# The key's norm, squared and on one side only, in an RWKV-7 and gMLP step

## The chip, the cores and the metric

The kernel runs on one core of one Trainium2 chip. The metric is the device time of one execution in microseconds (us), lower is better; the time before is the median of three runs. The engines are named as the profile names them: PE is TensorE (its weight loads are PEld), DVE is VectorE, ACT is ScalarE, POOL is GpSimd, SP is the engine that issues most DMAs.

## The reference

One layer of a backbone over 512 latent tokens and 128 context tokens, 2048 wide, in fp32: a modulated RMSNorm, one projection `w_in`, a bidirectional RWKV-7 time mixing on one half of the channels and a chunked gMLP on the other, `w_out`, and a SwiGLU feed-forward part. The change lies in the time mixing, in how the key `kk` is normalized for each head of 64 channels:

```python
kk = heads(k * lp['k_k'])
kk = kk * lax.rsqrt(jnp.maximum(jnp.sum(kk * kk, axis=-1, keepdims=True), 1e-24))
for d in range(2):
    decay = heads(jnp.exp(-jnp.exp(w_log)))
    a = jax.nn.sigmoid(lp['a0'][d] + ad @ lp['a2'][d])
    kd = heads(k * (1.0 + (a - 1.0) * lp['k_a']))
    y, s_fin = _delta_scan(rh, decay, kd, vh, -kk, kk * heads(a), s0[:, d], reverse=(d == 1))
# a step of the scan, with a_t = -kk and b_t = kk * a:
#   sa = S a_t ;  S = S * w_t + sa b_t^T + v_t k_t^T ;  y_t = S r_t
```

The normalized key enters the state only as the product of a reading (`S a_t`) and a writing (`sa b_t^T`) of the same token, so one factor of it can be moved from the one to the other.

## The kernel before, in words

All 640 tokens are columns of tiles with 128 channels on the partitions, so a tile of one channel block is 128x640. The kernel has four stages: modulation and norm; `w_in` with the preparation of both mixers; the recurrence over chunks of 64 tokens with `w_out`; and the feed-forward part, which is the longest. Big matmuls are fp32 split into a high and a low part, three matmuls for each block (L190 to L192), 320 columns wide; the high part is cast on ACT (L168), the low part subtracted on DVE (L169).

The change lies in the second stage. Blocks of 128 output columns of `w_in` come one after another, each in four pieces. When a block is done, `take` copies it to SBUF (L955) and puts a generator for it into the queue `mixA`: `take_r`, `take_v` and `take_k` for each of eight pairs of heads, `take_gv` and `take_gu` for each gMLP group. `between` is called after the matmuls of a block row and runs the queue by a budget. Each `yield x` of a generator says that x units of the budget are used up; how fast the queue is run follows from the cost that is still outstanding (`pace`, with `KCOST` = 50 for a `take_k`). Two more queues hold the solving of small triangular systems (`solve`, `merge`).

`take_k` does the following for a pair: it takes the shifted key `zk`, multiplies it by `k_k` into `nkk` (L565), squares that on ACT (L567), sums the squares of each head with a matmul by a matrix of ones (`pmm`, L519), bounds the sums from below (`ssq`, L570), takes the square root on ACT (L572) and the reciprocal on DVE in two halves (L576), and multiplies `nkk` by -1 and that (L578). Then, for each direction `d`, TensorE makes the low-rank products `pwa` (L592, L593), ACT their tanh (`sg` and `tha`, L596), DVE a running sum of `sg` (`L`, L604), ACT the exponentials of it (L607, L608). The reading rows `R` are `nkk` and `zr` times the exponential (L615, L618, L621); the writing rows `X` are `tha` times `nkk` (L632) and the key `f` times the inverse exponential (L636 to L640). TensorE multiplies them chunk by chunk into `pG` (L651), DVE masks the result into `GR` and `GA` (L660, L661), ACT copies part of it to `GB` (L655, L663), TensorE transposes `X` (`pXT`, L669; copies `XT`, L675) and makes `pW0` (L683). At the end `zv` is weighted by another product through `pmm` (L698). All of it goes to DRAM in `d_S` for the recurrence.

`nkk`, `ssq` and the others have one buffer each, apart from `t1` with two. The order of instructions on an engine follows the text only loosely: it is set when the program is built.

## Time and profile before

| | us |
|---|---|
| time, median of 3 runs (lowest to highest) | 3225.3 (3222.83 to 3228.34) |
| the profiled execution: time | 3226.49 |
| the profiled execution: span from first to last instruction | 3224.7 |
| TensorE busy | 3097.7 |
| VectorE busy | 2337.3 |
| ScalarE busy | 1460.7 |
| mean granted clock of TensorE | 0.990 |

The profile is of one execution. A line like `L572 ACT ACTIVATE ssq<-ssq x8: 737/740/742` gives the line of the kernel, the engine, the operation, the tile written and the tiles read, how many there were, and the shortest, median and longest duration in ns. In a list of waits, `PE pG L651 <- DVE X L636: 5.1, 8, 1.6` says that PE, ahead of the matmuls of L651 into `pG`, stood idle until DVE had written `X` in L636: 5.1 us in total, 8 times, 1.6 us at the longest.

### The profile page before, as it was taken

What the parts mean: (1) busy time and instruction counts of PE and PEld (TensorE: products, weight loads), DVE (VectorE), ACT (ScalarE), POOL (GpSimd) and SP (SyncE); (2) the same over time, 40 slices, a digit from 0 to 9 for tenths busy, and PEclk for the clock granted to TensorE, in tenths of its full rate; (3) what the DMA queues carried; (4) which work ended last, traced back from release to release, by engine and by line L of the source; (5) the groups of instructions that cost most, each with busy time, mean ns of one, the idle gap of its engine ahead of it and who ended that gap; (6) DMA issues with size and microseconds to landing.
All of it is one profiled execution on the core that took longest, in us unless ns stands there. A gap on an engine that the chain in (4) does not pass through costs nothing.

```text
span 3224.7 us, 72310 instructions
## 1 busy us (share of the span) xinstructions
PE 3097.7 (96%) x28216; PEld 2861.5 (89%) x28216; DVE 2337.3 (72%) x4107; ACT 1460.7 (45%) x3197; POOL 1215.7 (38%) x1065
## 2 busy tenths in 40 slices
PE   6999999999999999999999999999999999999997
PEld 4688778777878888899999999999999999999997
DVE  4547666676666677767877777778788688777778
ACT  3334444444444444346644444444444454444365
POOL 2001121211122023311366556656655645555542
PEclk9999999999999999999999999999999999999999
DMA  9667786777778688564534433343344364553453
GB/s 372 220 197 203 194 215 187 204 205 197 201 197 220 193 273 268 178 197 128 149 112 125 121 117 118 117 128 120 107 130 128 104 197 151 157 157 111 145 167 121
DMA packets 740438, 550.88 MB, mean 171 GB/s; under 512 B 141056, under 2 KB 673504, under 8 KB 731264
## 3 DMA queue, kind: packets, MB, share of 16 engines
q1 hardware_dynamic: 727136, 532.47, 55.5%
q0 software_dynamic: 10624, 13.23, 1.7%
q8 instruction: 222, 3.64, 0.5%
q14 instruction: 120, 0.98, 0.1%
q10 hardware_dynamic: 2336, 0.57, 0.1%
HBM read 437.79 MB, written 110.95 MB: 170 GB/s over the span
## 4 chain that ended last, share of the span: by engine, by line
PE 72%; DVE 10%; DMA 8%; issue 5%; ACT 3%; POOL 2%; SPq 0%; DVEq 0%; POOLq 0%; ACTq 0%
PE P L1640 15%; PE P L1638 15%; PE P L1639 15%; PE big L190 5%; PE big L192 4%; PE big L191 4%; DVE lo L1420 2%; DMA wt<-in_w_mod_dram 2%; PE pm L903 1%; PE pG L651 1%; DMA raw<-in_w_in_dram 1%; PE big L1035 1%; PE big L1479 1%; PE big L1478 1%; PE big L1480 1%
## 5 line engine op out<-in xcount | busy, mean ns | idle before, releaser
L1640 PE MATMUL P<-xo,lo 128*128 128x320 f32 x2352 | 727.9, 310 | 2.2 <-DVE lo L1420 2.1
L1638 PE MATMUL P<-xo,hi 128*128 128x320 f32 x2352 | 727.5, 309 | 0.7 <-ACT hi L1419 0.7
L1639 PE MATMUL P<-xo,hi 128*128 128x320 f32 x2352 | 727.4, 309 | 0.0
L1420 DVE TENSOR_TENSOR lo<-raw,hi 128x512 fp32r<-128x512 f32 x526 | 512.0, 977 | 164.8 <-ACT hi L1419 160.3
L1419 ACT CAST hi<-raw 128x512 fp32r<-128x512 f32 x526 | 327.7, 623 | 487.6 <-PE P L1639 393.5
L190 PE MATMUL big<-h_hi,hi 128*128 128x320 f32 x1376 | 450.4, 327 | 10.1 <-ACT hi L168 6.7
L1640 PEld LDWEIGHTS P<-xo,lo 128*128 128x128 f32 x2352 | 442.1, 188 | 3.2 <-DVE lo L1420 2.9
L1638 PEld LDWEIGHTS P<-xo,hi 128*128 128x128 f32 x2352 | 442.0, 188 | 1.0 <-ACT hi L1419 1.0
L1639 PEld LDWEIGHTS P<-xo,hi 128*128 128x128 f32 x2352 | 442.0, 188 | 0.0
L192 PE MATMUL big<-h_hi,lo 128*128 128x320 f32 x1376 | 433.8, 316 | 0.8 <-DVE lo L169 0.6
L191 PE MATMUL big<-h_lo,hi 128*128 128x320 f32 x1376 | 431.7, 314 | 0.5 <-DVE h_lo L352 0.5
L1548 POOL TENSOR_TENSOR raw<-raw 128x512 f32<-128x512 f32 x252 | 406.6, 1623 | 16.4 <-DVE lo L1420 4.9
L1640 PE MATMUL P<-xd,lo 128*128 128x320 f32 x1232 | 384.9, 312 | 16.3 <-DVE lo L1420 16.3
L1638 PE MATMUL P<-xd,hi 128*128 128x320 f32 x1232 | 383.4, 311 | 1.8 <-ACT hi L1419 1.1
L1639 PE MATMUL P<-xd,hi 128*128 128x320 f32 x1232 | 382.1, 310 | 0.0
L190 PEld LDWEIGHTS big<-h_hi,hi 128*128 128x128 f32 x1376 | 261.9, 190 | 79.0 <-issue 47.8
L169 DVE TENSOR_TENSOR lo<-raw,hi 128x512 fp32r<-128x512 f32 x268 | 183.3, 687 | 195.0 <-ACT hi L168 177.7
L1419 ACT CAST hi<-rawd 128x512 fp32r<-128x512 f32 (+1 forms) x288 | 168.7, 589 | 241.9 <-PE P L1639 201.7
L192 PEld LDWEIGHTS big<-h_hi,lo 128*128 128x128 f32 x1376 | 261.3, 190 | 9.5 <-issue 2.8
L191 PEld LDWEIGHTS big<-h_lo,hi 128*128 128x128 f32 x1376 | 261.8, 190 | 6.0 <-DVE h_lo L352 1.2
L168 ACT CAST hi<-raw 128x512 fp32r<-128x512 f32 x268 | 164.9, 619 | 223.8 <-PE big L191 115.8
L1640 PEld LDWEIGHTS P<-xd,lo 128*128 128x128 f32 x1232 | 232.4, 189 | 22.9 <-DVE lo L1420 22.7
(404 smaller groups left out, 6046.4 us busy)
## 6 DMA issues: line engine op xcount, KB each, us to landing
wt<-in_w_mod_dram SPq DMA_DIRECT2D x96, 1024.0 KB
raw<-in_w_ffn_gate_dram SPq DMA_DIRECT2D x182, 256.0 KB
raw<-in_w_ffn_up_dram SPq DMA_DIRECT2D x182, 256.0 KB
rec<-d_S SPq DMA_DIRECT2D x80, 576.0 KB
raw<-in_w_in_dram SPq DMA_DIRECT2D x172, 256.0 KB
rawd<-in_w_ffn_down_dram SPq DMA_DIRECT2D x128, 256.0 KB
raw<-in_w_out_dram SPq DMA_DIRECT2D x96, 256.0 KB
xd<-d_os SPq DMA_DIRECT2D x66, 320.0 KB
```

The costliest lines, as they stand in the source:

```text
L168: S.copy(hi, raw)
L169: V.tensor_sub(lo, raw, hi.bitcast(F32))
L190: TE.matmul(halves[hf], hi[:, k, :], h_hi[:, kb, s], start=(kb == 0), stop=False)
L191: TE.matmul(halves[hf], hi[:, k, :], h_lo[:, kb, s], start=False, stop=False)
L192: TE.matmul(halves[hf], lo[:, k, :], h_hi[:, kb, s], start=False, stop=(kb == KB - 1))
L651: in_turn([lambda cc=cc, h=h: TE.matmul(two[h][:, cc - c0, :], X[hsl(h), cc].rearrange("p s t -> p (s t)"), R[hsl(h), cc].rearrange("p s t ...
L1419: S.copy(hi[:, 0:nk], raw[:, 0:nk])
L1420: V.tensor_sub(lo[:, 0:nk], raw[:, 0:nk], hi[:, 0:nk].bitcast(F32))
L1548: G.tensor_tensor(out=o[:, 0:nk], in0=p[:, 0:nk], in1=q[:, 0:nk], op=ALU.subtract)
L1638: TE.matmul(ps, hi[:, k, :], xk[:, 0, :], start=f, stop=False)
L1639: TE.matmul(ps, hi[:, k, :], xk[:, 1, :], start=False, stop=False)
L1640: TE.matmul(ps, lo[:, k, :], xk[:, 0, :], start=False, stop=l)
```

## The change

The square root is left out, with its yield of 0.5. `nkk` takes the factor -1 at once and is not normalized; the reading rows use it as it is. The reciprocal is now that of the squared norm, and a new tile `nks` holds `nkk` times it; the writing rows use `nks` in place of `nkk`.

```diff
-        V.tensor_scalar_mul(nkk, zk, prm[:, C_KK + p:C_KK + p + 1])
+        V.tensor_scalar(nkk, zk, prm[:, C_KK + p:C_KK + p + 1], -1.0, op0=ALU.mult, op1=ALU.mult)
         sq = bk.tile([P, T], F32, tag="t1", name="sqk", bufs=2)
         S.activation(sq, nkk, AF.Square)
         yield 0.5
         ssq = bp.tile([P, T], F32, tag="t2", name="ssq", bufs=1)
         pmm([(bones, sq)], lambda ps, s: V.tensor_scalar_max(ssq[:, s], ps, 1e-24))
         yield 1.0
-        S.activation(ssq, ssq, AF.Sqrt)
-        yield 0.5
         for hf in range(2):
             s = slice(HALF * hf, HALF * hf + HALF)
             V.reciprocal(ssq[:, s], ssq[:, s])
             yield 2.0
-        V.scalar_tensor_tensor(out=nkk, in0=nkk, scalar=-1.0, in1=ssq, op0=ALU.mult, op1=ALU.mult)
+        nks = bk.tile([P, T], F32, tag="nks", name="nks", bufs=1)
+        V.tensor_mul(nks, nkk, ssq)
...
-            V.scalar_tensor_tensor(out=tha, in0=tha, scalar=1.0, in1=nkk, op0=ALU.add, op1=ALU.mult)
+            V.scalar_tensor_tensor(out=tha, in0=tha, scalar=1.0, in1=nks, op0=ALU.add, op1=ALU.mult)
```

## The prediction, made before the result was known

> **What bounds the kernel now.** I read the head of the profile's page first, then the table by stage, then what TensorE waits for in the stage that the change touches, and last the square root's own rows and one pair of heads in order of time.

> ```profile
> span 3224.7 us, 72310 instructions
> PE 3097.7 (96%) x28216; PEld 2861.5 (89%) x28216; DVE 2337.3 (72%) x4107; ACT 1460.7 (45%) x3197; POOL 1215.7 (38%) x1065
> ```

> TensorE (PE) is busy for 96% of the span; ScalarE (ACT), which loses the square root, for 45%. So work that leaves ACT counts only where TensorE stood still because of it. The root is taken once for each of the eight pairs of heads; its first and last use give the stage. The second fence is the table by stage (start:end, length, then busy time of PE, PEld, DVE, ACT, POOL, the granted clock, DMA share, GB/s).

> ```profile
> L567 ACT ACTIVATE sqk<-nkk x8: 737/740/741, 193.1 to 913.7; 128x640 f32<-128x640 f32 x8
> ```

> ```profile
> 193.00:1010.00 817.00, 778.56 (x9243) 647.95 (x9241) 546.93 (x1096) 382.74 (x838) 145.93 (x241) 0.99 0.74 201
> 1010.00:1100.00 90.00, 88.75 (x1253) 81.75 (x1252) 60.85 (x118) 43.55 (x83) 14.85 (x19) 1.00 0.63 180
> ```

> From the first root to the end of the last pair are 817 us, and TensorE stands still for 817.00 - 778.56 = 38.4 us of them. That is the most that any relief of ACT or VectorE (DVE) can bring here, as far as idle time shows it. The list of TensorE's waits in this stage says who ends them (total us, times, longest):

> ```profile
> PE pG L651 <- DVE X L636: 5.1, 8, 1.6
> PE pm L903 <- DMA wt<-in_w_mod_dram: 4.6, 5, 2.4
> PE pG L651 <- DVE GA L661: 3.5, 4, 2.1
> PE big L190 <- ACT hi L168: 3.2, 5, 1.0
> PE pXT L669 <- DVE GA L661: 2.8, 6, 0.7
> PE pmm L519 <- DVE zv L698: 2.8, 3, 2.0
> PE pXT L669 <- ACT XT L675: 2.7, 5, 0.7
> ...
> PE pW L683 <- ACT XT L675: 1.6, 2, 1.1
> PE pG L651 <- DVE X L640: 1.5, 2, 1.1
> PE pG L651 <- ACT hi L168: 1.2, 2, 0.7
> ...
> PE pXT L669 <- ACT GB L663: 0.7, 2, 0.3
> ...
> PE pG L651 <- ACT GB L663: 0.5, 2, 0.3
> ```

> No wait names the square root. The ones behind it in the chain of one pair are those for X (the writing rows, L636 and L640): 5.1 + 1.5 = 6.6 us in 10 waits. One step further on the same chain stand the masked products GA and the copies XT and GB: 3.5 + 2.8 + 2.7 + 1.6 + 0.7 + 0.5 = 11.8 us in 21 waits. The rest (modulation weights by DMA, casts of the big weights, zv of the pair before) does not hang on the root.

> **The change, part by part.** What goes, first the root's and the next tanh's line, then the two rows that wait around the root:

> ```profile
> L572 ACT ACT_TABLE_LOAD  x8: 1283/1283/1283, 193.9 to 918.1; - x8
> L572 ACT ACTIVATE ssq<-ssq x8: 737/740/742, 195.8 to 924.3; 128x640 f32<-128x640 f32 x8
> ```

> ```profile
> L596 ACT ACT_TABLE_LOAD  x8: 1283/1283/1283, 197.1 to 930.4; - x8
> ```

> ```profile
>   DVE ssq L570: 11.5, 8
>   ACT ssq L572: 4.0, 5
> ```

> ACT loses 8 roots x 0.740 = 5.9 us and 16 table loads x 1.283 = 20.5 us, together 26.4 us, and the 11.5 us in which it stood waiting for ssq: 4.7 us a pair. No other line of the stage loads a table, so both loads of a pair go with the root. DVE loses the 4.0 us of waiting for the root. Of the 26.4 us nothing is on TensorE's path by itself: ACT has 817 - 382.74 = 434 us free in the stage. If that cover were gone, all 26.4 would count; it is not.

> What is exchanged on DVE costs nothing by its nearest rows. The product with two factors in place of one (L565) stays a tensor-scalar operation, and a two-factor one of the same shape (L598) is no slower than today's; the new product nks = nkk x ssq replaces a three-operand one, and a plain product of that shape (L621) takes as long:

> ```profile
> L598 DVE TENSOR_SCALAR sg<-sg 128x640 f32<-128x640 f32 x16 | 7.9, 493 | 15.2 <-ACT sg L596 14.6
> ...
> L578 DVE SCALAR_TENSOR_TENSOR nkk<-nkk,ssq 128x640 f32<-128x640 f32 x8 | 6.5, 814 | 0.0
> ...
> L565 DVE TENSOR_SCALAR nkk<-zk,prm 128x640 f32<-128x640 f32 x8 | 4.6, 572 | 0.1
> ```

> ```profile
> L621 DVE TENSOR_TENSOR R<-zr,gam 128x640 f32<-128x640 f32 x16 | 13.1, 820 | 0.0
> ```

> The bounds: 8 x (493 - 572) = -0.6 us if both factors cost like constants, +0.0 if as today; 8 x (820 - 814) = +0.05 us for the product. I take 0. The two reciprocals stay, and so does their place ahead of everything else of the pair on DVE. The new tile is one more buffer with one slot; its next writer and its readers are all on DVE, so no engine gains a wait by it. A wait is not added but moved: the writing rows still come behind the reciprocals, the reading rows no longer need them, though DVE runs both in one queue.

> What counts is how much earlier X is finished. One pair in order of time (start, us, engine, line; in brackets the idle time before and what ended it), DVE and then ACT:

> ```profile
> 304.96 0.88 DVE L570 TENSOR_SCALAR ssq<-pmm 128x320 f32<-128x320 f32 x2
> 306.65 4.17 DVE L576 RECIPROCAL ssq<-ssq 128x320 f32<-128x320 f32 x2 [0.81 <-ACT ssq L572]
> ...
> 311.28 0.81 DVE L578 SCALAR_TENSOR_TENSOR nkk<-nkk,ssq 128x640 f32<-128x640 f32 x1
> 313.71 0.49 DVE L598 TENSOR_SCALAR sg<-sg 128x640 f32<-128x640 f32 x1 [1.62 <-ACT sg L596]
> 314.15 0.61 DVE L629 TENSOR_SCALAR fs<-tha,kah,ka 128x640 f32<-128x640 f32 x1
> 314.68 1.53 DVE L604 TENSOR_TENSOR_SCAN L<-scan,sg 128x320 f32<-128x320 bf16 x2
> ```

> ```profile
> 305.88 0.74 ACT L572 ACTIVATE ssq<-ssq 128x640 f32<-128x640 f32 x1 [0.26 <-DVE ssq L570]
> 309.47 0.62 ACT L168 CAST hi<-raw 128x512 fp32r<-128x512 f32 x1 [2.85 <-PE big L191]
> 310.11 1.28 ACT L596 ACT_TABLE_LOAD   x1
> 311.40 0.53 ACT L596 ACTIVATE sg<-pwa,w0h 128x320 f32<-128x320 f32 x1
> ...
> 313.15 0.53 ACT L596 ACTIVATE sg<-pwa,w0h 128x320 f32<-128x320 f32 x1 [0.48 <-PE pwa L593]
> ```

> Two things hold X back here. The reciprocal waits 0.81 us for the root. And the tanh stands behind the second load for 1.28 us, while DVE, done with L578 at 312.09, is idle for 1.62 us until sg comes. Without the root DVE gets through the reciprocals 0.8 us sooner; without the load the tanh comes up to 1.28 us sooner, less where TensorE's pwa products are themselves late. These overlap, so I put the lead at 0.8 to 2.1 us a pair (0.81 + 1.28 at most).

> Against it stands the removed "yield 0.5". Yields are the units in which the pair's work is dealt out between the big matmuls, so TensorE asks for the pair's products half a unit earlier. From 193.1 to 913.7 are 7 pairs, 102.9 us each. A pair's blocks yield about 2.6 + 5.1 + 50 units, and the four gating groups in these seven pairs 4 x 17 / 7 = 9.7 more: 67 units, hence 1.53 us a unit and 0.76 us for the half. The net lead is 0.8 - 0.76 = 0.04 us to 2.1 - 0.76 = 1.3 us; I take the middle, 0.67.

> The mean wait for X is 6.6 / 10 = 0.66 us, so such a lead wipes it out where it follows the root in the same direction of scan; the second direction is fifty us on, with DVE's idle time between, and gains little. By count I give the first direction 6 of the 10: 4 us. Of the 11.8 us for GA, XT and GB, which follow X, I give a quarter, since each has its own queue ahead of it: 3 us. Sum 7 us.

> On the load: the load ends at 310.11 + 1.28 = 311.39 and the tanh starts at 311.40, and it began 0.02 us after the cast ahead of it ended (309.47 + 0.62 = 310.09). [...]

> The profiled execution took 3226.49 us with a span of 3224.7; the median of the three runs is 3225.3, 1.2 below. Less 7 us the profiled execution comes to 3219.5, the median to 3218.3.

> **The rivals.** *Asked too early (slower).* The half unit moves every product of a pair forward on TensorE by 0.76 us, but the lead reaches only what hangs on the root. The waits of the list that do not (GA 10, XT 7, GB 4, casts 7, zv 3, modulation weights 5: 36 waits) each grow by up to 0.76 us, 27 us at the end of the scale; with somewhat under half of it, +12 us, the median is 3237. For it: TensorE's waits are many and short, about 1 us, which is the sign of products asked for just before they are ready. Against it: the dealing out follows remaining work, so half a unit in 67 may be made up. It decides from the point where the stage's idle time of TensorE passes 38.4 + 6.5 = 45 us.

> *Hidden anyway (no change).* The lead is only the lower end, 0.04 us, and the waits stay: 3225. For it: no wait of TensorE's list names the root. The same time would come if the table loads stayed because another function of the stage turned out to need its own table; against that, only these two lines load one today.

> **How the numbers follow.** About 0.2%, 6.5 us, is what a measurement of this kernel can tell from no change. The forecast has a chance of 0.53, with a range of its own from -2 us (half of the X waits of the first direction) to -14 us (all X waits of 6.6 and over half of the 11.8): 3211 to 3223. Of it I put 0.41 beyond 6.5 us and 0.12 within. Asked too early has 0.39, of which 0.36 beyond 6.5 us and 0.03 within; hidden anyway has 0.08, all within. That makes faster 0.41, same 0.23, slower 0.36. The range that should hold 8 in 10 goes from 3212, near the forecast's lower end, to 3238, just over the slower rival's price.

> **What would show it.** Right: no table load at the tanh's line, ACT's busy time down by about 26 us, DVE's reciprocal starting at once after ssq; the waits for X down from 6.6 to about 2.5 us and TensorE's idle time in the stage down to about 31 us; the later stages merely shifted. Wrong: X waits unchanged or larger with the loads gone (the lead was eaten by the earlier asking), idle time of TensorE over 45 us, or a difference that arises behind the stage, after 1100 us. One thing lies outside my sum: the order on an engine is not that of the text (L629 runs ahead of L604 above), so the order of other instructions may come out differently once this chain is shorter, and the small waits fall elsewhere.

## The result: slower by 0.9%

The changed kernel takes 3255.8 us (median of 4 runs, 3251.3 to 3259.3) against 3226.8 us before on the same chip (four runs here, where the table above has three): a ratio of 1.0088, 95% interval 1.0074 to 1.0101, so about 29 us slower. The profile after, its head first and then the tanh's own rows:

```profile
span 3249.6 us, 72295 instructions
PE 3107.8 (96%) x28216; PEld 2864.5 (88%) x28216; DVE 2317.3 (71%) x4107; ACT 1434.5 (44%) x3173; POOL 1219.7 (38%) x1065
```

```profile
L595 ACT ACTIVATE sg<-pwa,w0h x32: 502/527/535, 198.2 to 992.0; 128x320 f32<-128x320 f32 x32
L595 ACT ACTIVATE tha<-pwa,w0h x32: 516/527/533, 198.6 to 992.7; 128x320 f32<-128x320 f32 x32
```

The change does what it says: no table load stands at the tanh any more, ACT is busy 1460.7 - 1434.5 = 26.2 us less, DVE's wait for the root is gone. And the kernel is slower. The table by stage, cut at the last big matmul of the second stage (1089 us before, 1115 us after), shows where; before, then after:

```profile
193.00:1089.00 896.00, 856.38 (x10415) 719.22 (x10414) 599.18 (x1196) 417.85 (x904) 159.59 (x259) 0.99 0.73 198
1089.00:3225.00 2136.00, 2080.94 (x16776) 2025.14 (x16774) 1647.17 (x2709) 977.68 (x2187) 1036.82 (x769) 0.99 0.49 150
```

```profile
193.00:1115.00 922.00, 869.83 (x10418) 724.68 (x10417) 598.42 (x1196) 393.26 (x879) 156.80 (x258) 0.98 0.72 193
1115.00:3250.00 2135.00, 2080.04 (x16778) 2023.76 (x16776) 1628.46 (x2710) 976.05 (x2189) 1043.38 (x770) 0.99 0.49 150
```

The stage with the change is 26 us longer; what follows takes 2136 and 2135 us. TensorE does the same matmuls in it (10415 and 10418 in the trace) and stands still for 922.00 - 869.83 = 52.2 us instead of 896.00 - 856.38 = 39.6: 12.6 us. The rest is in the clock, 0.98 for 0.99: the trace's record of it has half speed (0.50) for 37.5 us of this stage after and for 13.7 us before, which is at most 23.8 / 2 = 11.9 us of lost work, or 9.7 us if only the time counts in which TensorE was busy at half speed (32.7 and 13.3 us). So 22 to 24.5 of the 26 us are found. The clock is no accident of one trace: its mean is 0.983 to 0.987 in the four runs of the changed kernel, and 0.988 to 0.992 in the 17 runs of the kernel before that stand beside e1.

TensorE's waits in this stretch, the lines that answer to those of before:

```profile
PE big L190 <- ACT hi L168: 11.2, 7, 3.2
PE pG L650 <- DVE X L635: 7.9, 11, 2.2
PE pmm L519 <- ACT Z L684: 5.5, 4, 2.3
...
PE pG L650 <- DVE X L639: 1.1, 2, 0.8
PE pG L650 <- DVE X L638: 0.3, 1, 0.3
```

The big matmuls now wait 11.2 us for their own weights' casts (hi, 4.4 before with the two of L651), those for X went up from 6.6 to 9.3 us, those of pmm for Z from 0.9 to 5.5. Set against each other by the big matmuls done, the changed kernel is level to within 3 us up to 432 us, then falls back 15 us to 487 us, of which 5 come back by 500 us, loses another 8 us little by little up to 960 us, and 12 us between 985 and 1040 us. The two large steps lie in the third pair and in the last, each time where the pair turns from its first direction to its second. The last pair there, ACT in order of time, before and after:

```profile
973.77 0.26 ACT L675 COPY XT<-pXT 128x128 f32<-128x128 f32 x1
973.92 0.42 ACT L955 COPY praw<-big 128x320 f32<-128x320 f32 x1
974.24 0.63 ACT L168 CAST hi<-raw 128x512 fp32r<-128x512 f32 x1
975.11 0.85 ACT L685 COPY Z<-pW 64x320 f32<-64x320 f32 x2 [0.24 <-PE pW L683]
975.86 0.52 ACT L596 ACTIVATE sg<-pwa,w0h 128x320 f32<-128x320 f32 x1
976.29 0.61 ACT L168 CAST hi<-raw 128x512 fp32r<-128x512 f32 x1
...
979.87 0.74 ACT L607 ACTIVATE gam<-L 128x640 f32<-128x640 f32 x1 [1.36 <-DVE L L604]
```

```profile
988.70 0.26 ACT L674 COPY XT<-pXT 128x128 f32<-128x128 f32 x1
988.85 0.43 ACT L954 COPY praw<-big 128x320 f32<-128x320 f32 x1
990.03 0.85 ACT L684 COPY Z<-pW 64x320 f32<-64x320 f32 x2 [0.75 <-PE pW L682]
990.78 0.52 ACT L595 ACTIVATE sg<-pwa,w0h 128x320 f32<-128x320 f32 x1
...
995.40 0.74 ACT L607 ACTIVATE L<-L 128x640 f32<-128x640 f32 x1
996.04 0.19 ACT L608 COPY gend<-gam 128x10 f32<-128x10 f32 x1
996.14 0.61 ACT L168 CAST hi<-raw 128x512 fp32r<-128x512 f32 x1
```

Before, the two casts of the next weights stand between the copies and the tanhs; after, they come behind the exponentials. The order of SP's loads (L167) goes with it. TensorE, meanwhile (in brackets its idle time and what ended it):

```profile
996.80 0.41 PE L190 MATMUL big<-h_hi,hi 128*128 128x320 f32 x1 [2.82 <-ACT hi L168]
997.05 0.30 PE L191 MATMUL big<-h_lo,hi 128*128 128x320 f32 x1
997.20 0.31 PE L190 MATMUL big<-h_hi,hi 128*128 128x320 f32 x1
997.34 0.31 PE L191 MATMUL big<-h_lo,hi 128*128 128x320 f32 x1
999.89 0.79 PE L650 MATMUL pG<-R,X 64*128 64x128 f32 x2 [2.24 <-DVE X L635]
```

It has only four big matmuls there to cover the pair's chain with, so it also reaches pG before X is there. What the root computed does not appear in these waits. What the trace shows is another order of the instructions that are left.

### The profile page after: what moved, and what is told of

Same layout as the page of the kernel before. It is cut to its first block, busy times and chain, and to the rows that moved or that the text cites. A ratio compares the mean times of both kernels' runs of the same rounds, so it can differ in the third digit from the quotient of the medians.

```text
span 3249.6 us, 72295 instructions
## 1 busy us (share of the span) xinstructions
PE 3107.8 (96%) x28216; PEld 2864.5 (88%) x28216; DVE 2317.3 (71%) x4107; ACT 1434.5 (44%) x3173; POOL 1219.7 (38%) x1065
## 4 chain that ended last, share of the span: by engine, by line
PE 73%; DVE 9%; DMA 7%; issue 5%; POOL 3%; ACT 2%; SPq 0%; DVEq 0%; POOLq 0%; ACTq 0%
PE P L1639 15%; PE P L1637 15%; PE P L1638 15%; PE big L190 5%; PE big L192 4%; PE big L191 4%; PE pm L902 1%; DMA wt<-in_w_mod_dram 1%; PE pG L650 1%; PE big L1479 1%; PE big L1478 1%; PE big L1477 1%; DVE lo L1419 1%; DMA mix<-dd 1%; PE big L1034 1%
## 5 line engine op out<-in xcount | busy, mean ns | idle before, releaser
L1419 DVE TENSOR_TENSOR lo<-raw,hi 128x512 fp32r<-128x512 f32 x526 | 497.9, 950 | 182.9 <-ACT hi L1418 178.2
L190 PE MATMUL big<-h_hi,hi 128*128 128x320 f32 x1376 | 450.3, 327 | 19.7 <-ACT hi L168 15.9
L191 PE MATMUL big<-h_lo,hi 128*128 128x320 f32 x1376 | 432.3, 314 | 0.7 <-DVE h_lo L352 0.7
L190 PEld LDWEIGHTS big<-h_hi,hi 128*128 128x128 f32 x1376 | 261.6, 190 | 87.8 <-issue 49.3
L169 DVE TENSOR_TENSOR lo<-raw,hi 128x512 fp32r<-128x512 f32 x268 | 183.6, 689 | 197.9 <-ACT hi L168 177.5
L168 ACT CAST hi<-raw 128x512 fp32r<-128x512 f32 x268 | 165.0, 618 | 243.3 <-PE big L191 134.2
L191 PEld LDWEIGHTS big<-h_lo,hi 128*128 128x128 f32 x1376 | 261.9, 190 | 8.9 <-issue 3.6
```

Of the source, the lines that this page charges most:

```text
L168: S.copy(hi, raw)
L169: V.tensor_sub(lo, raw, hi.bitcast(F32))
L190: TE.matmul(halves[hf], hi[:, k, :], h_hi[:, kb, s], start=(kb == 0), stop=False)
L191: TE.matmul(halves[hf], hi[:, k, :], h_lo[:, kb, s], start=False, stop=False)
L1419: V.tensor_sub(lo[:, 0:nk], raw[:, 0:nk], hi[:, 0:nk].bitcast(F32))
```

## The experiments

Times are medians; each ratio is to the kernel before on the same chip, with its 95% interval. The runs of one kernel lie up to 20 us apart (e14: 3228 to 3248), so a difference of a few us in one trace says little.

| kernel | us | ratio to before |
|---|---|---|
| changed | 3255.8 | 1.0088 (1.0074 to 1.0101) |
| e1: changed, yield 0.5 back | 3257.9 | 1.0094 (1.0079 to 1.0109) |
| e2: before, yield taken out | 3236.8 | 1.0032 (1.0022 to 1.0043) |
| e3: before, yield 0.6 | 3235.0 | 1.0032 (1.0020 to 1.0044) |
| e4: changed, yield 1.0 | 3244.9 | 1.0060 (1.0042 to 1.0078) |
| e5: changed, yield 0.5, dead root | 3225.6 | 1.0005 (0.9990 to 1.0019) |
| e6: changed, yield 0.5, dead square | 3228.8 | 1.0013 (1.0002 to 1.0025) |
| e7: changed, casts first everywhere | 3276.5 | 1.0159 (1.0144 to 1.0174) |
| e8: before, casts first everywhere | 3282.9 | 1.0185 (1.0170 to 1.0200) |
| e9: changed, five pieces earlier | 3240.5 | 1.0046 (1.0032 to 1.0059) |
| e10: before, same pieces later | 3235.8 | 1.0034 (1.0020 to 1.0048) |
| e11: changed, all pieces 60 earlier | 3240.4 | 1.0049 (1.0036 to 1.0062) |
| e12: changed, all pieces 150 earlier | 3234.0 | 1.0029 (1.0015 to 1.0043) |
| e13: changed, yield 0.5, five pieces | 3238.4 | 1.0042 (1.0029 to 1.0054) |
| e14: changed, no yield, dead root | 3237.5 | 1.0042 (1.0027 to 1.0056) |

**The yield.** The first theory (A) was the prediction's slower rival: half a unit less per pair moves the work forward.

```diff
         yield 1.0
+        yield 0.5          # e1; 1.0 in e4
         for hf in range(2):
# e2, in the kernel before (0.6 in e3):
         S.activation(ssq, ssq, AF.Sqrt)
-        yield 0.5
```

> The changed kernel with the yield of 0.5 put back where the root stood; the root stays out. Theory A (the half unit less per pair moves the pair's work forward against the big matmuls, and the stage falls into stalls): back to the time of before or a little under it, 3218 to 3230 us, TensorE's idle time between 193 us and the last big matmul of the stage about 38 us. Theory B (the shorter chain without the root gives another order on the engines, whatever the yield): stays near 3255 us, with the long waits for the casts (hi, L168) still there.

> The kernel before, root and both table loads kept, only the yield of 0.5 behind the root taken out. Theory A: slower by most of the change's loss, 3245 to 3262 us. Theory B: as before, 3222 to 3232 us.

> The kernel before with the yield behind the root at 0.6 in place of 0.5: nothing computed differs, only the dealing out is shifted by a tenth of a unit. If the loss is a steady effect of asking early (theory A), this is the same or up to 5 us faster, 3220 to 3228 us. If any shift of the dealing lands in another set of stalls (theory C: the time depends on where the pieces fall, without direction), it can be off by 10 us or more to either side, most likely slower: 3230 to 3255 us.

> The changed kernel with a yield of 1.0 in the root's place, half a unit more than before had. Theory A: asked later still, so at or below the first experiment, 3212 to 3228 us. Theory B: near 3255 us. Theory C: no order between this one and the one with 0.5; anywhere from 3220 to 3260 us.

Putting the yield back brings nothing (3257.9), so theory A falls as the cause of the loss. A whole unit (e4) is 13 us better than half a unit, 3244.9, which neither A (3212 to 3228) nor B (near 3255) had expected. With the root in place the same yield does count: without it 3236.8, 11 us slower, between the ranges of A and B. But a shift of a tenth of a unit the other way costs 9 us too (3235.0), so it is not that asking earlier is bad and later good. The kernel before stands at a favourable place, and a small step to either side of it cost about 10 us. In e1 and e4 the last pair's casts stand behind the exponentials as in the changed kernel; in e2 and e3, which have the root, they do not.

**Dead work in the root's place.** So the root as an entry in the program, not as arithmetic, was the next suspect. The operation writes into the tile of the squares, which nobody reads again.

```diff
         yield 1.0
+        S.activation(sq, ssq, AF.Sqrt)     # e5; AF.Square in e6
+        yield 0.5                          # not in e14
         for hf in range(2):
```

> The changed kernel, yield of 0.5 put back, and the square root back on ACT at its place and with its table loads, but as dead work: it writes into a tile that nobody reads, so it is on no chain. Theory B1 (the loss comes from the order in which the casts of the next big weights are put on ACT and their loads on SP; with a root in the program the order is that of before, two casts ahead of the exponentials of the last pair's second direction, where the changed kernel has none): back near before, 3218 to 3236 us, TensorE's wait for hi (L168) in the stage about 4 us instead of 8 to 11. Theory B2 (the loss is in what the data do: reading rows of another size, a product on DVE, the chain itself): stays at 3250 to 3260 us.

> As the dead root, but the dead operation is a Square, which needs no table load: 8 x 0.74 us on ACT and no loads. Its order has two casts ahead of the exponentials of the last pair's second direction, but is not that of before elsewhere. Theory B1: clearly below the changed kernel, 3222 to 3242 us. Theory B2: 3250 to 3260 us. If only the table loads' time mattered (they keep the pair back), it is like the changed kernel, 3250 us or more.

> The changed kernel as it is, without the yield, and only the dead square root added on ACT. With the yield the dead root gave the time of before. If the yield is a term of its own of about 11 us, as it was in the kernel before: 3232 to 3241 us. If it counts only together with the missing root: 3220 to 3230 us. Theory B2 (the data's chain) would have 3250 us and is not expected.

With 26 us of useless work on ACT, root and table loads, the changed kernel is back at the time of before (1.0005, interval across 1), about 30 us below e1, from which its program differs by that work alone. The profile of e5:

```profile
193.00:1094.00 901.00, 863.93 (x10414) 724.88 (x10413) 598.78 (x1196) 417.19 (x904) 159.94 (x259) 0.98 0.72 197
```

```profile
PE pG L652 <- DVE X L637: 5.2, 8, 1.8
...
PE big L190 <- ACT hi L168: 3.0, 5, 0.7
```

TensorE's idle time is 901.00 - 863.93 = 37.1 us, the waits for X and hi are those of before, and ACT's order at the last pair's turn is again cast, Z, tanh, cast. In fact the whole order is back. Set side by side in the traces, from 193 us to the last big matmul, TensorE, DVE, POOL and SP's DMA issues go through the same sequence as before, and on ACT only 8 copies `R<-nkk` of 881 instructions (root and loads aside) stand at another place. The data go through the changed arithmetic (key as it is, `nks`, no root in it). That settles that the arithmetic costs nothing beyond what the interval leaves open.

It does not settle what a shorter chain is worth, for the dead root is not off the chain, as I had expected. The reciprocal overwrites `ssq`, which the dead root reads, and waits for it. DVE's wait (us, times) ahead of its work on `ssq`, until the dead root ends:

```profile
  ACT sqk L572: 10.7, 5
```

Before, it waited 4.0 us for the root. On average over the pairs, the first write of X begins 21.7 us after the start of the square in e5, 21.4 before and 20.1 in the changed kernel. No run has the short chain in the order of before.

The dead square, without any table load (ACT is busy for 397.70 us of the stage, against 417.19 in e5), comes within about 4 us of before, so the time of the loads is not needed for that. Its order is not that of before: 768 of ACT's 881 instructions stand in the same sequence, in the changed kernel 747. So another order need not cost 29 us. Here a part of my expectation missed: only one cast stands among the last pair's copies and tanhs, and the next one behind the exponentials, much as in the changed kernel:

```profile
976.78 0.74 ACT L608 ACTIVATE gam<-L 128x640 f32<-128x640 f32 x1 [1.39 <-DVE L L605]
977.55 0.74 ACT L609 ACTIVATE L<-L 128x640 f32<-128x640 f32 x1
...
978.61 0.62 ACT L168 CAST hi<-raw 128x512 fp32r<-128x512 f32 x1
```

TensorE does not wait for hi there, only 3.0 us for X, so a late cast does not cost by itself. Over the stage this kernel waits 4.2 us for hi, as before, and 6.8 us for Z (0.9 before), yet loses little; its clock stays at 0.99 where e1's is 0.97 with little more idle time:

```profile
193.00:1096.00 903.00, 858.22 (x10423) 719.88 (x10423) 601.95 (x1198) 397.70 (x889) 159.22 (x259) 0.99 0.72 197
```

```profile
193.00:1118.00 925.00, 875.20 (x10423) 733.46 (x10422) 599.12 (x1197) 392.71 (x881) 158.10 (x259) 0.97 0.71 192
```

Idle time is 44.8 us in the one and 49.8 in the other, 5 us apart; half speed holds for 13.7 us in the one and 61.4 in the other, worth up to 24 us. Together that is more than the 22 us by which the stages differ, so half of the half-speed time is an upper price. Without the yield (e14) the dead root is 12 us slower than with it, the size that e2 found: with a root in the program the yield is a term of its own.

**The casts moved.** `split` loads, casts and subtracts a piece of `w_in`; a precedence in the planner's ranking moves it forward (or back, where negative).

```diff
             b, q = pieces[n]
-            parts[n] = split(w_in[0, q * 512:(q + 1) * 512, blocks[b][0]:blocks[b][0] + P], 4)
+            with tc.high_priority():       # e7, e8; offset=60 in e11, 150 in e12
+                parts[n] = split(w_in[0, q * 512:(q + 1) * 512, blocks[b][0]:blocks[b][0] + P], 4)
# e9, e13: offset=150, e10: offset=-150, only for n in (68, 69, 70, 152, 153)
```

> The changed kernel, unaltered in what it computes and deals out, but the loads, casts and low parts of the w_in pieces are given precedence over the pair's work where both are ready. Theory B1: TensorE's waits for hi go to under 4 us in the stage and the time to 3215 to 3240 us. Theory B2: no gain, 3250 us or more. It can also cost, since the loads stand earlier in SP's queue and may hold up the stores behind them: then the waits move from hi to GA and XT.

> The kernel before with the same precedence for loads and casts, to tell its own effect. Theory B1: before has little to gain (4.4 us of waits for hi), so 3215 to 3240 us, and the gap between this kernel and the changed one with the same precedence is under 10 us, where without it it is 29 us. Theory B2: the gap stays near 29 us.

> The changed kernel with five of the 172 w_in pieces moved forward in the order: pieces 68 to 70 and 152 to 153, whose casts stand behind the exponentials of the second direction in the third and the last pair, where before they stand ahead of them. Nothing else is touched. Theory B1 (these late casts, and the half-clock stretches behind the stalls that they make, are the loss): the two steps of 12 to 14 us at these places go, and the time falls to 3225 to 3236 us. Theory B3 (the late casts are only one sign of a generally worse order): at most a third of the loss comes back, 3245 us or more.

> The kernel before with the same five pieces moved back in the order; in it this moves the casts of pieces 152 and 153 behind the last pair's exponentials, as in the changed kernel, while 68 to 70 keep their place. Theory B1: slower by the one step, 8 to 14 us, so 3232 to 3240 us. Theory B3: as before, 3220 to 3230 us.

> The changed kernel with all w_in pieces moved forward a little (60 places in the planner's ranking, where the full precedence of the earlier experiment put them ahead of everything). Theory B1: most of the loss back, 3220 to 3238 us, and no long hole in the casts. Theory B3: anywhere, more likely 3240 us and above.

> As the one with 60 places, with 150: the casts ahead of each pair's exponentials are in number almost those of before. Theory B1: 3215 to 3235 us, and if the root's 26 us of ACT are worth anything to TensorE, below the kernel before. Theory B3: 3240 us and above, towards the 3277 us of full precedence.

> The changed kernel with both: the yield of 0.5 put back and the five pieces (68 to 70, 152 and 153) moved forward. The five alone left 16 us of the loss, the yield alone all of it. If what is left is the yield's part, which a root in its place had shown as 11 us (theory B1 with A as a second, smaller term): 3224 to 3234 us. If what is left is spread over many other places of the order (theory B3): 3236 to 3245 us, as with the five alone.

Full precedence was the wrong remedy: the waits for hi go, but TensorE now waits longer for the loads of the modulation weights, and stands idle ahead of other matmuls. The waits of e7:

```profile
PE pm L902 <- DMA wt<-in_w_mod_dram: 13.6, 11, 3.3
PE pblk L842 <- issue: 7.9, 5, 2.8
```

Both kernels lose, to 3276.5 and 3282.9 us, more than I had allowed. What B1 said of the gap holds: with the same precedence the changed kernel is no longer the slower one. Both orders are quite other ones than those of before and after, so this says only that the loss does not belong to the arithmetic.

Five pieces moved (e9) bring 13 of the 29 us back, and the two places can be seen to heal: between 432 and 500 us it falls back 4 us instead of 11, and the last pair's turn costs 2 us instead of 12. The longest wait for hi goes from 3.2 to 1.2 us:

```profile
PE pG L650 <- DVE X L635: 5.9, 11, 1.8
...
PE big L190 <- ACT hi L168: 3.7, 5, 1.2
```

The counterpart (e10) names the same five pieces in the kernel before; in its trace pieces 68 to 70 keep their place, those of the last pair and some behind them come later, and it costs 11 us. It puts the stall there:

```profile
977.62 0.41 PE L190 MATMUL big<-h_hi,hi 128*128 128x320 f32 x1 [3.02 <-ACT hi L168]
980.70 0.79 PE L651 MATMUL pG<-R,X 64*128 64x128 f32 x2 [2.23 <-DVE X L636]
```

These are the two stalls of the changed kernel, 2.82 and 2.24 us there, made in a kernel that still has its root, its loads and its yield. So late pieces (load, cast and low part moved together, and no run parts them) are shown as a cause, worth 11 us where they were made alone and just under half of the loss where they were taken away. They are not the only way to lose: e1 waits for hi at most 0.9 us at a time in its third pair, yet falls back 16 us between 420 and 500 us, with 24 us at half speed there. Moving all pieces by 60 places gives the time of e9 (3240.4); by 150 places it leaves 9 us (3234.0), so that with nothing but the order changed 20 of the 29 us come back. Adding the yield to the five (3238.4) gives no more than the five alone. e9, e11 and e13 miss their ranges for a full recovery by 2 to 5 us, and e12 lies just inside its own. The 9 us that remain are of the size that e2 and e3 lost by small shifts; that they are spread over the other differences in order is likely, but not shown. No kernel here is faster than before; e5 only equals it.

## Why the prediction was wrong, step by step

- *The costs on ACT and DVE*: right. 26.4 us were forecast to leave ACT, 26.2 left. The exchanged DVE operations cost nothing: DVE has 599.2 us before and 598.4 us after in the stage.
- *Nothing of it on TensorE's path by itself*: right. e5 carries all 26 us and is as fast as before.
- *The lead*: right. X's first write of a pair begins 20.1 us after the square, 1.3 us sooner than before (21.4), inside the forecast 0.8 to 2.1; the first pG begins 0.9 us sooner, near the 0.76 taken for the yield. But e1, which has the yield, asks 0.7 us sooner too, so the yield is not the reason.
- *What the lead takes off the waits for X (the 7 us)*: this is the step that failed. X was to go from 6.6 to 2.5 us and went to 9.3; TensorE's idle time was to fall by 7 us and rose by 12.6. In the first direction, where the lead was to act, X's waits are 2.4 us in 5 waits before (not 4 us in 6, as the sum had it) and 2.3 in 6 after; in the second they went from 4.2 to 7.1 us. The sum took the order on the engines as given and asked only when each result is ready. The prediction named a new order as outside its sum and gave it no price and no case of its own, and by the experiments most of the loss came from there.
- *The clock*: missing from the sum. A stall was priced at its own length; about 10 to 12 of the 26 us are half speed behind stalls.
- *Asked too early*: right in sign, and the idle time did pass the 45 us it named, but the mechanism was not the one at work: the yield put back (e1) changed nothing. Where the root stays, the yield is worth 11 to 12 us (e2, e14), near the 12 us that the rival was priced at, yet e3 shows a loss in the other direction too, so the agreement is luck as far as these runs show. The waits for GA, XT and GB stood on both sides: in the forecast they follow X and share its lead, in this rival the lead does not reach them.
- *Hidden anyway*: right that the root's time was hidden and that the arithmetic costs nothing (e5), wrong that the waits stay.

## What to carry to other kernels

In a kernel where a planner sets the order on the engines from the program's own operations, taking out an operation is two changes: the work that goes, and a new order of all that is left; the second can be much the larger when the bound engine has many short waits. Before crediting a saving, compare the new order on the queues that feed the bound engine (here the weights' casts on ACT and their loads on SP), and test the arithmetic alone by putting dead work in the place of what went; then see in the trace whether the old order is back, and what waits for the dead work. A small shift that computes nothing new, such as e3's tenth of a unit, tells how favourable the present order is, and so how much any edit has to bring to pay.

## What the runs showed of the hardware that I had not expected

The two stalls of about 3 us (3.17 and 2.82) cost more than their length. The granted clock around the two places of the changed kernel (start:end, length, busy times of PE, PEld, DVE, ACT and POOL, then the clock, DMA share and GB/s):

```profile
442.00:449.20 7.20, 4.03 (x27) 2.59 (x25) 4.88 (x8) 6.33 (x14) 0.00 (x0) 1.00 0.91 232
449.20:456.00 6.80, 4.83 (x20) 2.37 (x18) 6.63 (x10) 1.02 (x3) 0.00 (x0) 0.50 0.82 246
456.00:463.00 7.00, 7.00 (x58) 6.35 (x57) 6.74 (x14) 2.45 (x6) 0.00 (x0) 1.00 0.71 177
992.00:998.70 6.70, 2.83 (x17) 1.18 (x15) 6.00 (x9) 4.16 (x9) 0.00 (x0) 1.00 1.00 296
998.70:1005.50 6.80, 4.84 (x19) 2.62 (x20) 5.66 (x9) 1.10 (x2) 0.00 (x0) 0.50 0.64 176
1005.50:1012.00 6.50, 6.50 (x64) 5.89 (x66) 5.02 (x11) 2.67 (x6) 0.00 (x0) 1.00 0.74 179
```
